# The differential layer's first values projection on the unscaled residual

## The chip, the cores and the metric

The kernel runs on one core of one Trainium2 chip. A time is the device time of one launch in microseconds (us). Profiled times come from one execution that the hardware profiler recorded. The engines are PE (TensorE: matmuls, and PEld for the loads of their stationary operand), DVE (VectorE), ACT (ScalarE), POOL (GpSimd) and SP (SyncE, whose queue issues the loads).

## What is computed

The reference is a chain of two models on 256 tokens of width 1024: a first block (two mixers and a mixture of experts), then two adaLN layers. Layer 0 has a sparse attention, layer 1 a differential attention, and each ends in a feed-forward block. Each half of a layer starts with a norm whose scale and shift come from the condition vector `c`:

```python
mod = cond @ w_ada[i] + b_ada[i]                  # six vectors of 1024 for each layer
sh1, sc1, g1, sh2, sc2, g2 = split(mod, 6)
h = rms_norm(x, ln_mix_g[i]) * (1 + sc1) + sh1
x = x + g1 * mixer(h)
h = rms_norm(x, ln_mlp_g[i]) * (1 + sc2) + sh2
x = x + g2 * (square(relu(h @ w_mlp_in[i])) @ w_mlp_out[i])
```

The differential mixer projects `h` to queries, keys and values (1024 columns each, 8 heads of 128), norms and rotates queries and keys per head of 64, takes two softmaxes per head and multiplies their weighted difference with the values. All data are fp32.

The change rests on an identity. With r the reciprocal root of one token's mean square, `h = r * (x * gain) + bias`, where `gain` and `bias` do not depend on the token. So `h @ W = r * ((x * gain) @ W) + bias @ W`: a projection can run on `x * gain` before r is known, and `bias @ W` comes out of it if `bias` is one more token.

## The kernel before

**Layout.** The residual `res` lies transposed in SBUF, 8 chunks (`KD`) of 128 features by 256 tokens. Each fp32 operand of a large product is split in a high and a low fp32r half (`hi`, `lo`), and a product is three passes: hi with hi, hi with lo, lo with hi. The activations' halves are `hT_hi` and `hT_lo`. The same memory, seen as `hX`, has 258 columns to a chunk: 256 tokens, the bias column, and a zero.

**Weights.** `load` (L131) puts 1 MB tiles into a ring of 8 slots, in program order on SP's queue. ScalarE casts the high half (`whi`, L151) and VectorE subtracts for the low half (`wlo`, L152), each 128x1024 at a time, with three buffers.

**Two forms of projection.** `proj_steps` (L461) has activations as the stationary operand and weights as the moving one: 8 chunks x 2 halves of tokens x 3 passes, 512 columns each; the result has tokens on the partitions. `proj_X_steps` (L440) has weights stationary and `hX` moving: 8 chunks x 4 blocks of 128 outputs x 3 passes, 258 columns each; the result is transposed, and its column 256 is `bias @ W`.

**Norms.** `closing` (L526) is the end of a block: for each of four pairs of chunks it adds the product to `res` times the gate, squares the result for the sums, and lets PE sum the squares over the partitions (`ssps`, `Stats.count`). There are two ways on from there.
- `Stats.rstd` and `normed`: VectorE prepares the mean, GpSimd takes the power -1/2, PE spreads the factor over the partitions (`rbps`, L358), and then each chunk is scaled (`nf`, L366), rounded to `hT_hi` (ACT, L372) and subtracted to `hT_lo` (L373). Only then can a projection start. `Stats.fill` puts adaLN products (`adaps`, L187) into PE's queue at that place.
- `Stats(plain=True)` with `feeding` (L394): each pair is written to `hX` as `res * gain` during the closing, the following product runs on it by `proj_X_steps`, `Stats.scale` makes the factor beside it as an SBUF tile `rb` and the results are scaled afterwards. Both feed-forward blocks (`mlp`, L1718) start in this way; the counts of the last two pairs and `scale` stand behind the fourth of the eight steps of their first product.

**adaLN vectors.** There are twelve, each 4 loads of 1 MB. They are made in halves on PE (`ada_half`, `fill`), or on VectorE (`ada_vector`, one load of 1 MB to a call, two operations of 128x1024, L256 and L258; after the fourth call PE sums over the partitions, 8 records). A feed-forward block calls `ada_vector` beside its products as long as fewer than `vectors` are done: 11 in the first, 12 in the second.

**The differential layer.** After the first feed-forward block, `modulated` (L2189) does the first of the two ways. `dproj(0)` (L2205) projects keys, queries and values of heads 0 to 3, in this order, each into two PSUM banks (`dps`). Norm, rope and transposes of keys and queries (`dheads`) are chains: generators that go on by one stage when a given number of projection steps has been issued. `dv` is copied from PSUM. Then `attention` runs over 8 units (heads): scores, exponentials and their difference for one unit, transposes of the weights (`ptps`, L1711) and the product with the values (`dob`) of the unit before. Into the first four units `work` puts the steps of `dproj(1)` (heads 4 to 7), and from the seventh on the first half of the output product (`oearly`); `olate` is its second half.

**Order.** Program order is priority. A planner with a simulated time line fixes the order on each engine ahead of the run; an engine then works through its queue in that order. PSUM has 8 banks, 4 of the pool `acc` and 4 of the pool `mm`.

Of the kernel before, what the change touches and what calls it, by code (L numbers as in the profile page):

```python
# [25 lines left out]
P = 128  # L26
T = 256
# [17 lines left out]
def block_kernel(ctx: ExitStack, tc: tile.TileContext, A: dict, out: bass.AP):  # L45
# [10 lines left out]
    def mm(shape=(P, 512), name="mm"):  # L56
        return mm_pool.tile(list(shape), F32, tag="mm", name=name)

    def acc(shape=(P, 512), name="acc"):
        return acc_pool.tile(list(shape), F32, tag="acc", name=name)  # L60

    def sc(shape=(P, 512), name="sc"):
        return scratch.tile(list(shape), F32, tag="sc", name=name)
# [49 lines left out]
    def col(name, i=0, n=None):  # L113
        g, r, k = where[name]
        return vcols[g][:, r + i : r + i + (k - i if n is None else n)]
# [278 lines left out]
    def feeding(gain, bias):  # L394

        hi, lo = hX
        for t in hX:
            nc.vector.memset(t.bitcast(F32)[:, :, T + 1 : TX], 0.0)
        b = bias[:, :, None]
        nc.vector.tensor_copy(hi[:, :, T : T + 1], b)  # L400
        nc.vector.tensor_tensor(lo[:, :, T : T + 1], b, hi[:, :, T : T + 1].bitcast(F32), op=ALU.subtract)

        def feed(pr):
            for k in (2 * pr, 2 * pr + 1):
                g = gain[:, k : k + 1]
                nc.scalar.activation(hi[:, k, 0:T], res[:, k, :], AF.Copy, scale=g)
                nc.vector.scalar_tensor_tensor(
                    lo[:, k, 0:T], res[:, k, :], g, hi[:, k, 0:T].bitcast(F32), op0=ALU.mult, op1=ALU.subtract
                )

        return feed
# [28 lines left out]
    def proj_X_steps(w, c0, outs):  # L440

        for k0, t in colblock(w, c0, 512):
            for k1, hi, lo in halves(t):
                for kk in range(hi.shape[1]):
                    k = k0 + k1 + kk
                    for h in range(4):
                        for i, (a, b) in enumerate(passes((hi, lo), hX)):
                            nc.tensor.matmul(  # L448
                                outs[h],
                                a[:, kk, h * P : (h + 1) * P],  # L450
                                b[:, k, :],
                                start=(k == 0 and i == 0),
                                stop=(k == KD - 1 and i == 2),
                            )
                    yield
# [70 lines left out]
    def closing(banks, gate=None, st=None, each=None, feed=None):  # L526

        def after(pr):  # L530
            v = add_pair(pr, banks[pr], gate)
            last = pr == KD // 2 - 1
            if feed is not None:
                feed(pr)
                st.square(pr, v)
                if pr >= 2:
                    st.count(pr - 2)
                return
            if st is not None:
                if last and st.w is not None:  # L540
                    held["first"]["dve"] = added[0]
                st.square(pr, v)
            if st is not None:
                for p in range(pr - 2, pr + 1 if last else pr - 1):
                    if last and p == pr and st.w is None:
                        st.fill()
                    if p >= 0:
                        st.count(p)
            if each is not None:
                for p in range(pr - 1, pr + 1 if last else pr):  # L550
                    if p >= 0:
                        each(p)

        return after
# [1084 lines left out]
    def modulation(lay, part, ln):  # L1639

        v = 6 * lay + part
        ada_until(v + 2)
        a = small.tile([P, KD], F32, tag="moda", name="moda")
        nc.vector.tensor_scalar(a, mods[v + 1], 1.0, None, op0=ALU.add)
        nc.vector.tensor_tensor(a, a, ln, op=ALU.mult)
        return a, mods[v]

    def modulated(st, lay, part, ln):
        normed(st.rstd(), *modulation(lay, part, ln))
# [68 lines left out]
    def mlp(lay, close, st, vectors):  # L1718

        ada_sum = ct("adasum", (P, D), tag="klo")  # L1720
        if ada_at[1]:
            ada_half()
        w_i, w_o = A["w_mlp_in_2"][lay], A["w_mlp_out_2"][lay]
        pend = None
        for j in range(9):
            rate[0] = 0.0
            if j < 8:
                hp = [(mm if j else acc)((P, TX), name="hp") for _ in range(4)]
                for n, _ in enumerate(proj_X_steps(w_i, j * 512, hp)):
                    if j == 0 and n == 3:  # L1730
                        st.count(2)
                        st.count(3)
                        rb = st.scale()
                both = n8("hid", F32R).rearrange("p (a k t) -> p a k t", a=2, k=4)
                for i in range(2):
                    r = sc((P, 2, T), name="relu")
                    b = pw.tile([P, 4], F32, tag="nm", name="hb")
                    for c in range(2):
                        nc.vector.tensor_copy(b[:, c : c + 1], hp[2 * i + c][:, T : T + 1])
                        nc.vector.tensor_tensor(r[:, c, :], hp[2 * i + c][:, 0:T], rb, op=ALU.mult)  # L1740
                        nc.scalar.activation(r[:, c, :], r[:, c, :], AF.Relu, bias=b[:, c : c + 1])
                    hi = both[:, 0, 2 * i : 2 * i + 2, :]
                    nc.scalar.activation(hi, r, AF.Square)
                    nc.scalar.activation(r, r, AF.Square)
                    nc.vector.tensor_tensor(both[:, 1, 2 * i : 2 * i + 2, :], r, hi.bitcast(F32), op=ALU.subtract)
                for _ in range(2):
                    if j and ada_at[0] < vectors:
                        ada_vector(ada_sum)
            if j == 0:
                banks = [acc((P, 2, T), name="mlp") for _ in range(4)]  # L1750
            if pend is not None:
                jj, bb = pend
                if jj == 7:
                    ada_close()
                    ada_until(6 * lay + 6)
                for c in (0, 2):
                    if c == 2 and ada_at[0] < vectors:
                        ada_vector(ada_sum)
                    after = close(banks) if jj == 7 and c == 2 else None
                    rows(w_o, jj * 4 + c, banks, (bb[:, 0], bb[:, 1]), c, jj == 0 and c == 0, after)  # L1760
            pend = (j, both)
# [420 lines left out]
    nlam = const.tile([P, 1], F32, name="nlam")  # L2182
    nc.vector.tensor_tensor(nlam, ls[:, 1:2], ls[:, 0:1], op=ALU.subtract)
    nc.vector.tensor_scalar(nlam, nlam, -lam_init, None, op0=ALU.add)
    st = Stats()
    mlp(0, lambda banks: closing(banks, mods[5], st), st_x, 11)


    modulated(st, 1, 0, col("lnx", 8, 8))  # L2189
    w_d = A["diff_w_in_2"][0]  # L2190
    dqT = ct("dqT", (P, KD, T), tag="t16")
    dv = ct("dv", (P, 2, D), tag="kv8")
# [3 lines left out]
    def dheads(ps, i, tabs, gain, dst, name):  # L2196
        n = ct("qn", (P, 2, 8, 64), tag=f"on{i}")
        for m in range(2):
            head_norm(ps[m], 8, n[:, m])
        rope(n, tabs, 8)  # L2200
        yield 8
        heads_T(n.rearrange("p m h d -> p m (h d)"), dst[i], gain)
        ready.add((name, i))

    def dproj(i):  # L2205

        for c0, tabs, gain, dst, name in ((1024, rt_dk, g_dk, dkT, "dk"), (0, rt_dq, g_dq, dqTs, "dq")):
            ps = [acc(name="dps") for _ in range(2)]
            yield from proj_steps(w_d, c0 + i * 512, ps)
            chains.add(dheads(ps, i, tabs, gain, dst, name))  # L2210
        ps = [acc(name="dps") for _ in range(2)]
        yield from proj_steps(w_d, 2048 + i * 512, ps)
        for m in range(2):
            nc.scalar.copy(dv[:, m, i * 512 : (i + 1) * 512], ps[m])
        ready.add(("dv", i))
# [25 lines left out]
    deps = {}  # L2241

    def diff_out(h, p):
        assert ("dv", h // 4) in ready
        pt = weights_T(p)
        yield
        j = h % 2
        if j == 0:
            dob[h // 2] = acc((P, 2, 2, P), name="dob")
        o = dob[h // 2]  # L2250
        vc = slice(h * P, (h + 1) * P)
        nc.tensor.matmul(o[:, j, 0, :], pt[:, 0:P], dv[:, 0, vc], start=(j == 0), stop=False)
        nc.tensor.matmul(o[:, j, 1, :], pt[:, P:T], dv[:, 0, vc], start=False, stop=False)
        nc.tensor.matmul(o[:, j, 1, :], pt[:, T : 3 * P], dv[:, 1, vc], start=False, stop=(j == 1))
# [91 lines left out]
```

## Time and profile before

| | us |
|---|---|
| runs: median of 3 (lowest, highest) | 1309.24 (1307.48, 1309.24) |
| the profiled execution | 1306.74 |
| its span | 1305.0 |
| PE busy | 1263.6 (97%) |
| DVE busy | 652.6 (50%) |
| ACT busy | 512.6 (39%) |
| first feed-forward block ends, first `dps` projection starts | 979.29, 988.21 |

The span is the time from the first to the last instruction in the profile. A busy share is an average over stages with different limits; what an edit is worth is read in its own stage. Matmuls are pipelined: the records of two that follow each other overlap, and the distance of their starts is what one costs PE. An fp32 matmul has two records, an fp32r matmul one. The granted clock is given as a part of the full 2.4 GHz.

### The profile page before, as it was taken

How to read it: one execution, taken by the hardware profiler on the slowest of the kernel's cores; microseconds unless marked ns; L12 is line 12 of the kernel's file. 1: busy time of each engine (PE TensorE's matmuls, PEld its weight loads, DVE VectorE, ACT ScalarE, POOL GpSimd, SP SyncE). 2: the span in 40 equal slices, each digit the busy share in tenths (PEclk: the TensorE clock that was granted, in tenths of full speed). 3: DMA queues.
4: the chain of work that ended last, by engine and by line, in shares of the span. 5: the costliest groups of instructions: out<-in, count | busy, mean ns of one | idle time of the engine just before them, and what ended most of it. 6: DMA issues, size and time to landing. Idle time of an engine off the chain costs nothing.

```text
span 1305.0 us, 22821 instructions
## 1 busy us (share of the span) xinstructions
PE 1263.6 (97%) x9471; PEld 1001.2 (77%) x9471; DVE 652.6 (50%) x1268; ACT 512.6 (39%) x918; POOL 68.4 (5%) x92
## 2 busy tenths in 40 slices
PE   8999899999999999999999999999999999999998
PEld 7779565665555555556886679999997779999998
DVE  6765310220101111105786777688766777655554
ACT  7743210111101111104555646545444565654644
POOL 1010000000000000000410000000001221000000
PEclk9999999999999999998999999999999999999999
DMA  7997799999999999998545846699677432555510
GB/s 252 369 411 302 305 421 420 420 421 421 422 420 420 421 421 421 420 413 296 186 156 193 323 140 212 206 353 338 244 256 259 161 130 76 180 173 187 194 66 33
DMA packets 99157, 373.98 MB, mean 287 GB/s; under 512 B 10649, under 2 KB 14442, under 8 KB 74730
## 3 DMA queue, kind: packets, MB, share of 16 engines
q1 hardware_dynamic: 99050, 372.49, 74.8%
q8 instruction: 76, 1.25, 0.4%
q14 instruction: 31, 0.25, 0.1%
HBM read 371.41 MB, written 1.05 MB: 285 GB/s over the span
## 4 chain that ended last, share of the span: by engine, by line
PE 74%; issue 11%; DVE 2%; ACT 1%; POOL 0%; DVEq 0%; ACTq 0%; POOLq 0%
PE hp L448 14%; PE mlp L491 14%; PE gups L1413 12%; PE dps L1443 6%; PE dps L469 5%; PE sums L1461 3%; PE gps L1367 2%; PE oearly L584 2%; PE qp L469 2%; PE olate L491 2%; PE adaps L187 1%; PE kv L469 1%; PE opair L2098 1%; PE kcv L469 1%; PE ptps L2089 1%
## 5 line engine op out<-in xcount | busy, mean ns | idle before, releaser
L152 DVE TENSOR_TENSOR wlo<-w,whi 128x1024 fp32r<-128x1024 f32 (+1 forms) x222 | 269.7, 1217 | 158.0 <-ACT whi L151 155.9
L151 ACT CAST whi<-w 128x1024 fp32r<-128x1024 f32 (+1 forms) x222 | 230.4, 1042 | 249.3 <-PE hp L448 105.6
L1413 PE MATMUL gups<-w,xg 128*64 128x256 f32 x2048 | 233.7, 381 | 3.8 <-PEq L1271 2.8
L1413 PEld LDWEIGHTS gups<-w,xg 128*64 128x64 f32 x2048 | 145.1, 137 | 90.0 <-issue 19.4
L491 PE MATMUL mlp<-hid,whi 128*128 128x256 f32 x1024 | 184.0, 282 | 0.0
L491 PEld LDWEIGHTS mlp<-hid,whi 128*128 128x128 f32 x1024 | 157.2, 188 | 0.4 <-issue 0.4
L491 PE MATMUL mlp<-hid,wlo 128*128 128x256 f32 x512 | 144.8, 283 | 0.0
L448 PE MATMUL hp<-hT_lo,whi 128*128 128x258 f32 x512 | 144.0, 282 | 0.0
L448 PE MATMUL hp<-hT_hi,whi 128*128 128x258 f32 x512 | 143.7, 283 | 0.0
L448 PE MATMUL hp<-hT_hi,wlo 128*128 128x258 f32 x512 | 142.5, 282 | 0.0
L1425 DVE TENSOR_TENSOR h<-h,gups 128x256 f32<-128x256 f32 x32 | 13.5, 421 | 235.7 <-ACT h L1424 235.7
L1443 PE MATMUL dps<-w,hT 128*64 128x512 f32 x496 | 112.7, 596 | 5.0 <-ACT hT L1433 5.0
L491 PEld LDWEIGHTS mlp<-hid,wlo 128*128 128x128 f32 x512 | 96.4, 188 | 1.6 <-issue 1.6
L448 PEld LDWEIGHTS hp<-hT_lo,whi 128*128 128x128 f32 x512 | 96.7, 189 | 0.0
L448 PEld LDWEIGHTS hp<-hT_hi,whi 128*128 128x128 f32 x512 | 96.1, 188 | 0.0
L448 PEld LDWEIGHTS hp<-hT_hi,wlo 128*128 128x128 f32 x512 | 95.9, 189 | 0.0
L1424 ACT ACTIVATE h<-gups 128x256 f32<-128x256 f32 x32 | 12.3, 383 | 181.4 <-PE gups L1413 181.4
L1443 PEld LDWEIGHTS dps<-w,hT 128*64 128x64 f32 x496 | 34.1, 137 | 64.3 <-issue 53.0
L1454 DVE COPY ysb<-dps 64x512 f32<-64x512 f32 x31 | 21.2, 683 | 107.1 <-PE dps L1443 107.0
L1455 ACT COPY ysb<-dps 64x512 f32<-64x512 f32 x31 | 18.0, 581 | 139.1 <-DVE ysb L1454 139.1
L1461 PE MATMUL sums<-sw,ysb 128*128 128x256 f32 x256 | 61.3, 385 | 6.3 <-DVE ysb L1454 6.3
L286 POOL TENSOR_TENSOR rs_r<-rs_t,mhalf 128x8 f32<-128x8 f32 (+2 forms) x24 | 36.5, 1521 | 486.4 <-DVE rs_t L280 481.3
(537 smaller groups left out, 2038.4 us busy)
## 6 DMA issues: line engine op xcount, KB each, us to landing
w<-in_w_gate_dram SPq DMA_DIRECT2D x64, 1024.0 KB
w<-in_w_up_dram SPq DMA_DIRECT2D x64, 1024.0 KB
w<-in_w_down_dram SPq DMA_DIRECT2D x62, 1024.0 KB
w<-in_w_ada_dram SPq DMA_DIRECT2D x48, 1024.0 KB
w<-in_w_mlp_in_dram SPq DMA_DIRECT2D x32, 1024.0 KB
w<-in_w_mlp_out_dram SPq DMA_DIRECT2D x32, 1024.0 KB
w<-in_diff_w_in_dram SPq DMA_DIRECT2D x12, 1024.0 KB
w<-in_w_in_dram SPq DMA_DIRECT2D x10, 1024.0 KB
```

The lines of the kernel that those rows point to most:

```text
L151: nc.scalar.copy(hi, v)
L152: nc.vector.tensor_tensor(lo, v, hi.bitcast(F32), op=ALU.subtract)
L286: nc.gpsimd.tensor_tensor(r, t, m, op=ALU.pow)
L448: nc.tensor.matmul(outs[h], a[:, kk, h * P : (h + 1) * P], b[:, k, :], start=(k == 0 and i == 0), stop=(k == KD - 1 and i == 2),)
L469: nc.tensor.matmul(outs[m], b[:, k, m * P : (m + 1) * P], a[:, kk, :], start=(k == 0 and i == 0), stop=(k == KD - 1 and i == 2),)
L491: nc.tensor.matmul(outs[dc // 2][:, dc % 2, :], a[:, 0, dc * P : (dc + 1) * P], b[:, a0 + kk, :], start=(first and kk == 0 and i == 0 and ...
L584: nc.tensor.matmul(banks[h // 2][:, h % 2, :], a[:, kk, h * P : (h + 1) * P], b[:, k, :], start=(k == 0 and i == 0 and h % 2 == 0), stop=( ...
L1367: nc.tensor.matmul(ps[:, j, :], part[:, m, k * P : (k + 1) * P], hot[:, m].rearrange("p e s -> p (e s)"), start=(n == 0), stop=(n == 3),)
L1413: nc.tensor.matmul(ps[j * 64 : (j + 1) * 64, s * 256 : (s + 1) * 256], xg[:, k, s0 : s0 + SLOTS], w[k // 4][:, k % 4, j * 256 : (j + 1) * ...
L1443: nc.tensor.matmul(dps[half * 64 : (half + 1) * 64, :], hT[:, c, j * 64 : (j + 1) * 64], dt[f // 2][:, f % 2, half * 512 : (half + 1) * 51 ...
L1454: nc.vector.tensor_copy(t[e2 * 64 : e2 * 64 + 64, 0:512], dps[0:64, :])
L1461: nc.tensor.matmul(sums[k // 2][:, k % 2, :], t[:, k * P : (k + 1) * P], sw, start=(pr == 0 and k % 2 == 0), stop=(after is not None and k ...
```

## The change

The first feed-forward block now ends as the sparse attention does: its closing feeds `res * gain` into `hX`, with the gain and bias of the differential layer's first norm. `dproj(0)` starts with the values of heads 0 to 3, by `proj_X_steps`, into two `acc` and two `mm` banks (`dvT`); behind its fourth step stand the last two counts and `scale`. Then `normed` writes `hT_hi` and `hT_lo` from `res` for the other projections. `dvalues` scales each bank by `rb` (DVE) and adds the bias column (ACT), transposes the result back in eight PE transposes, and copies it to `dv`. Keys and queries follow as before, and there is no values projection at the end of `dproj(0)`. The `fill` calls of this norm are gone with `rstd`. In `diff_out` the assertion that the values are there has become a wait of the program's order (`need`).

```diff
-    st = Stats()
-    mlp(0, lambda banks: closing(banks, mods[5], st), st_x, 11)
-    modulated(st, 1, 0, col("lnx", 8, 8))
+    st = Stats(plain=True)
+    norm_d = []
+    def close_0(banks):
+        norm_d.extend(modulation(1, 0, col("lnx", 8, 8)))
+        return closing(banks, mods[5], st, feed=feeding(*norm_d))
+    mlp(0, close_0, st_x, 11)
...
+    def dvalues(ps, rb):
+        vT = []
+        for i in range(2):
+            v = sc((P, 2, T), name="vT")
+            b = pw.tile([P, 4], F32, tag="nm", name="vb")
+            for c in range(2):
+                p = ps[2 * i + c]
+                nc.vector.tensor_copy(b[:, c : c + 1], p[:, T : T + 1])
+                nc.vector.tensor_tensor(v[:, c, :], p[:, 0:T], rb, op=ALU.mult)
+                nc.scalar.activation(v[:, c, :], v[:, c, :], AF.Identity, bias=b[:, c : c + 1])
+            vT.append(v)
+        yield 2
+        for i in range(2):
+            t = mm((P, 2, 2, P), name="tps")
+            for m in range(2):
+                for c in range(2):
+                    nc.tensor.transpose(t[:, m, c, :], vT[i][:, c, m * P : (m + 1) * P], ident)
+            nc.scalar.copy(dv[:, :, 2 * i * P : (2 * i + 2) * P].rearrange("p m (c d) -> p m c d", c=2), t)
+        ready.add(("dv", 0))
+
     def dproj(i):
+        if i == 0:
+            ps = [f((P, TX), name="dvT") for f in (acc, acc, mm, mm)]
+            for n, _ in enumerate(proj_X_steps(w_d, 2048, ps)):
+                if n == 3:
+                    st.count(2)
+                    st.count(3)
+                    norm_d.append(st.scale())
+                yield
+            rb = norm_d[2]
+            normed(rb, *norm_d[:2])
+            chains.add(dvalues(ps, rb))
         for c0, tabs, gain, dst, name in (...):
...
+        if i == 0:
+            return
         ps = [acc(name="dps") for _ in range(2)]
         yield from proj_steps(w_d, 2048 + i * 512, ps)
...
-        assert ("dv", h // 4) in ready
+        need(("dv", h // 4))
```

## Rows read from the trace of the kernel before

**Rows 1.** The page: busy us, share of the span, instructions of each engine.
```profile
PE 1263.6 (97%) x9471; PEld 1001.2 (77%) x9471; DVE 652.6 (50%) x1268; ACT 512.6 (39%) x918; POOL 68.4 (5%) x92
```

**Rows 2.** Stretches: bounds, length, busy us by engine, granted clock, DMA share, GB/s.
```profile
802.00:979.00 177.00, 176.99 (x1495) 174.07 (x1495) 133.38 (x183) 93.17 (x131) 0.00 (x0) 1.00 0.77 274
979.00:988.20 9.20, 8.25 (x88) 4.84 (x86) 5.57 (x13) 4.50 (x8) 1.62 (x1) 0.81 0.67 224
...
1034.20:1070.70 36.50, 36.50 (x183) 28.63 (x182) 29.12 (x73) 21.16 (x52) 10.28 (x5) 1.00 0.36 116
1070.70:1112.40 41.70, 39.85 (x307) 37.10 (x307) 31.77 (x77) 25.04 (x62) 3.87 (x3) 1.00 0.30 102
```

**Rows 3.** Chain of waits, 970 to 1110 us: start, us, what.
```profile
979.29 0.79 PE ssps L328 x8
...
984.01 0.90 PE rbps L358 x4
984.91 3.31 PE adaps L187 x32
988.21 29.92 PE dps L469 x128
1018.13 0.87 PE tps L391 x8
```

**Rows 4.** Groups of 979 to 988.2 us: busy us, mean ns, idle before.
```profile
L187 PE MATMUL adaps<-w,cond 128*32 128x256 f32 x64 | 5.5, 490 | 0.0
```

**Rows 5.** Time line, `olate` to first feed-forward block: start, us, what, idle before.
```profile
786.37 0.28 PE L491 MATMUL olate<-oT,wlo 128*128 128x256 f32 x1
...
796.70 1.67 POOL L286 TENSOR_TENSOR rs_r<-rs_t,mhalf 128x2 f32<-128x2 f32 x1 [109.29 <-DVE rs_t L280]
...
800.82 0.37 ACT L352 COPY rb<-rbps 128x256 f32<-128x256 f32 x1 [2.08 <-PE rbps L358]
...
801.06 0.16 DVE L1739 COPY hb<-hp 128x1 f32<-128x1 f32 x1 [0.64 <-PE hp L448]
801.22 1.42 DVE L1740 TENSOR_TENSOR relu<-hp,rb 128x256 f32<-128x256 f32 x4
```

**Rows 6.** The same before the second feed-forward block: the power.
```profile
1121.94 0.69 POOL L286 TENSOR_TENSOR rs_r<-rs_t,mhalf 128x2 f32<-128x2 f32 x1 [21.27 <-DVE rs_t L280]
```

**Rows 7.** Time line of the normed chunks before and during `dk`.
```profile
984.94 1.26 DVE L366 SCALAR_TENSOR_TENSOR nf<-res,moda,rbps 128x256 f32<-128x256 f32 x3 [1.21 <-PE rbps L358]
985.46 1.31 ACT L372 ACTIVATE hT_hi<-nf,mod 128x256 fp32r<-128x256 f32 x3 [2.92 <-DVE nf L366]
...
996.05 0.48 DVE L373 SCALAR_TENSOR_TENSOR hT_lo<-nf,mod,hT_hi 128x256 fp32r<-128x256 f32 x1
```

**Rows 8.** One `ada_vector` sum on PE; its DVE operation, min/median/max ns.
```profile
L258 DVE SCALAR_TENSOR_TENSOR adasum<-w,cond,adasum x35: 1276/1280/1289, 764.0 to 951.0; 128x1024 f32<-128x1024 f32 x35
...
837.70 0.64 PE L187 MATMUL adaps<-adasum,ones 128*32 128x256 f32 x8
```

**Rows 9.** SP's queue, 940 to 1100 us: issue, us to landing, loads.
```profile
942.71 9.99 SPq L131 DMA_DIRECT2D w<-in_w_ada_dram  x4
954.00 51.66 SPq L131 DMA_DIRECT2D w<-in_diff_w_in_dram  x12
```

**Rows 10.** Time line of `dq`'s last rope step, its transposes, scores, `ptps`.
```profile
1023.02 0.42 DVE L1671 TENSOR_TENSOR qn<-qn,rtmp 128x256 f32<-128x256 f32 x1
...
1028.11 1.03 PE L391 MATMUL tps<-ident,qn 128*128 128x128 f32 x8
...
1034.18 0.70 PE L1690 MATMUL scores<-dkT,dqT 64*128 64x256 f32 x2
...
1077.23 0.30 PE L1711 MATMUL ptps<-ident,p 128*128 128x128 f32 x1 [1.25 <-DVE deps L2231]
```

**Rows 11.** Stretches of PE alone: length, busy us, granted clock, DMA.
```profile
985.00:986.00 1.00, 1.00 (x12) 0.50 1.08 393
...
1077.00:1078.00 1.00, 0.77 (x4) 1.00 0.00 0
```

## Prediction

> **What bounds the kernel now.** I read the page's busy times first: TensorE (PE) is busy for 97% of the span [rows 1], so an edit pays only if it takes work from PE's queue or removes time in which PE waits. The table of stretches comes next [rows 2]. Inside the first feed-forward block (802 to 979 us) PE is busy for 176.99 of 177 us. Between 979.0 and 988.2 it is busy for 8.25 of 9.20 us at a mean granted clock of 0.81, and this is the stretch that the change attacks. From 1034.2 to 1070.7 PE has no idle time, and from 1070.7 to 1112.4, the later half of the attention, it has 1.85 us. The chain of waits shows what stands between the feed-forward block and the first projection [rows 3]: sums of squares, the adaLN tiles that `Stats.fill` puts there as filling, GpSimd's power, a spread of the factor, more adaLN tiles, and at 988.21 us the first `dps` matmul. By the table of groups the filling is 64 `adaps` records, 5.5 us of PE [rows 4]. So the stretch is no bare wait: 5.5 us of its 8.9 are work that has to be done somewhere.
>
> **The handover, before.** The last matmul of the block ends at 979.29 and the first projection starts at 988.21: 8.92 us. The values projection of the first heads then costs, later on, 8 x 2 x 3 = 48 matmuls; 128 of that kind took 29.92 us [rows 3], 0.234 each, so 11.2 us. Together 20.1 us.
>
> **The handover, after.** The new order is the one in which `out_late` and the first feed-forward block already meet: feeding, 96 matmuls of 258 columns, the counts inside them, the spread near their end. That place is in the trace [rows 5]. Its last `olate` matmul starts at 786.37 and by its own duration ends at 786.65; the first reader of the last bank starts at 801.06 after waiting for PE. That is 14.4 us for the 96 matmuls, 24 records of the sums and the spread, with PE in work throughout. I take 14.4 for the values projection in its new place. To it come:
> - 4 more records of the sums before the block's end (8 against 4, as `plain` counts both halves); 8 cost 0.79 us [rows 3]: +0.4.
> - The first `dk` matmul now needs a normed chunk, and that needs the factor `rb`. The copy of `rb` starts at 800.82, while the projection ends at about 801.0 [rows 5]. Copy 0.37, one `nf` (1.26/3 = 0.42) and its rounding on ScalarE (1.31/3 = 0.44 [rows 7]) make 1.2 us from the copy's start, to 802.0: PE waits 1.0 us. GpSimd's power ahead of the copy took 1.67 us there and 0.69 before the second block [rows 5, 6]; with the short one all could come 1.0 sooner, and PE would wait for nothing. I take 0.7, near the upper end, for the close of this block is the one in which the power was long.
> - Eight transposes of `vT`, 16 records: the same kind took 0.87 us for 8 [rows 3], so +1.7.
> - VectorE's pace during `dk`: before, it began the chunks 3.2 us ahead of PE (984.94 against 988.21) and wrote the last `hT_lo` by 996.5 [rows 7], about 1.5 us before PE came to that chunk. Now it starts some 2 us closer to PE and also scales four banks, 1.42 us for four in the same form [rows 5]; against that, its share of the split weights for `dk`'s first half is done during the values projection, where it is free. Between 0 and 2 us of waiting; I take 0.4.
> - The bias columns, `vb` copies and the four bias additions are on VectorE and ScalarE beside PE's 11 us of `dk`, and the two copies into `dv` replace the two of before: nothing on the path. Without that cover they would cost the four scalings' 1.4 us again.
>
> The sum: 14.4 + 0.4 + 0.7 + 1.7 + 0.4 - 20.1 = -2.5 us.
>
> **What is moved.** Without `fill`, the last of the twelve adaLN vectors is open when the diff layer ends, so the second feed-forward block makes it with `ada_vector`, as the first block did for five. Four 1 MB loads leave SP's queue between 942.71 and 952.7, ahead of the twelve loads of `diff_w_in` that begin at 954.00 [rows 9], and go in among the second block's weights. `diff_w_in` so starts four ring slots earlier, and those slots are no longer held until PE has read the adaLN tiles at 988. No row shows PE waiting for `diff_w_in`, so I count nothing. In the second block VectorE gets 8 operations, seven of 1.28 us [rows 8]; the first block carries five times that and keeps PE full [rows 2], which hides them. PE gets 8 records of 0.64 us together [rows 8]: +0.6. Were ScalarE's or VectorE's order disturbed there, it would cost up to one such operation. The total is now -1.9.
>
> **The attention.** The values projection used to be PE's work while the queries `dq` went through norm, rope and transposes: `dq`'s last rope step ends at 1023.4, its transposes run at 1028.11, the first scores at 1034.18 [rows 10]. After, the second half's projections fill that time, so 11.2 us of filling are missing further on. The 36.5 us from 1034.2 to 1070.7 have no PE idle, and VectorE is busy for 29.12 of them [rows 2]. PE's work there shrinks to 36.5 - 11.2 = 25.3 us; VectorE's must shrink by 4 as well, or it becomes the bound. It does where the splits and head norms of the second half move ahead of the first scores with their matmuls, so it fits, tightly. Bounds: a gain of the 1.85 us of idle behind it, if the second heads are ready earlier; a loss of all 11.2 if this part is paced by its latency and not by PE. I take +0.4, near the first, since PE was full there. In all **-1.5 us**.
>
> **Profile against the runs.** The profiled execution took 1306.74 us, its span 1305.0 and 1.7 around it; the median of the runs is 1309.24, 2.5 higher. The sum is a difference made in the profiled execution: 1305.2 for that one, and 1307.7 against the median.
>
> **The skill against the trace.** In 985 to 986 us the granted clock is 0.50 [rows 11], which is 1.2 GHz; PE had just run the narrow sums and waited for GpSimd's power. Around 1077, after full matmuls, a wait of 1.25 us left it at 1.00, 2.4 GHz [rows 10, 11]. The Trainium skill ("TensorE: Matmul & The Clock Gate", Part 1) says that the throttled state is the default and that activity releases it. By that rule a wait before `dk` could bring the low level back, which is the third rival below; by the row of 1077 it does not.
>
> Of the two powers (1.67 us at 796.70, 0.69 at 1121.94), the first ran beside an operation of VectorE of 1.28 us, a kind with two inputs from SBUF [rows 8]. The Trainium skill ("GPSIMD Engine Reference", Specifications) says that GpSimd shares its SBUF interfaces with VectorE and that instructions with two SBUF inputs contend; the rows agree. By the long power the wait before `dk` is 1.0 us, by the short one zero.
>
> **Rivals.**
> - *The attention gets shorter too.* The second heads' keys and queries are projected where the values were, so their norms are ready before units 4 to 7 ask. For it: 1.85 us of idle there; the transposes run 4.7 us after their data is written, so the planner's order has slack. Against: those units also wait on VectorE. Price: handover with no wait (-0.7) and no slow chunk (-0.4), and half of the idle gone with nothing lost (-1.3): -3.9 us, 1305.3.
> - *The attention runs out of filling* (slower). Eleven us of matmuls that could run at any time are gone from in front of it; when `dproj(1)` ends early, PE stands in front of `ptps` as at 1077, where it waited 1.25 us for VectorE [rows 10], but at each of six units. It decides once the added idle passes 4.5 us; six waits of 1.25 are 7.5: -1.9 + 7.5 = +5.6, 1314.8. Against: PE's idle there was zero until 1070.
> - *The clock falls at the handover.* the 3.3 us of adaLN tiles from 984.91 to 988.21 [rows 3] lie in that level; as long a stretch of `dk` at half the speed would do 1.65 us less: -1.5 + 1.65 = +0.2, 1309.4. Against: the row of 1077.
> - *It does not do what it says*: `dk` waits for all eight chunks, some 7 us at 0.9 us of VectorE each. Before, `dk` started at 988.21, 7.8 us ahead of the last chunk's write [rows 3, 7], so I give it little; it would end at 1315.
>
> **How the numbers follow.** A change under 0.2%, 2.6 us, cannot be told from none: faster is below 1306.6, slower above 1311.9. Forecast 0.42, the low clock 0.05 (both within 0.2%); the shorter attention 0.35 (faster); the lack of filling 0.14 and the waiting `dk` 0.04 (slower). That is 0.35, 0.47 and 0.18. The range, 1303.0 to 1312.5, leaves out the far half of each outer case; the forecast's own range is 1306.6 to 1310.
>
> **What would show it.** In the changed trace: no `adaps<-w,cond` and no PE idle between the block's last matmul and 96 `dvT` matmuls; `rb` copied about as these end and the first `dps` matmul within 1.2 us; granted clock 1.00 throughout; ten-odd us less between `dq`'s end and the last `dps`; eight `adaps<-adasum` records in the second block. It is wrong if PE's idle between the first scores and `olate` grows by more than 2 us, or if the first `dk` matmul waits for more than two chunks.

## The result, and the profile after

The changed kernel took 1315.82 us (median of 4 runs, 1315.23 to 1316.85) beside 1308.36 us of the kernel before on the same chip (4 runs, 1307.45 to 1309.24): ratio 1.0061, 95% interval 1.0047 to 1.0075, so 7.5 us slower by the medians and 8.0 by the ratio. I had forecast 1307.7, 1.5 less than the median that I then had (1309.24), and 1312.5 as the upper end.

The page of the changed kernel: busy us, share of the span, instructions of each engine. It answers to [rows 1].

```profile
PE 1272.2 (97%) x9483; PEld 1011.7 (77%) x9483; DVE 664.4 (51%) x1291; ACT 517.4 (39%) x931; POOL 68.7 (5%) x92
```

TensorE (PE) is as full as it was, 97%. That share doesn't show what went wrong, because a matmul at half the clock counts as busy too. The table of stretches does. First the kernel before, cut at its own milestones: the end of the first feed-forward block, the first `dps`, the first scores, the first `olate` in the chain, the end. Columns as in [rows 2].

```profile
979.30:988.20 8.90, 7.95 (x84) 4.54 (x84) 5.36 (x12) 4.50 (x8) 1.62 (x1) 0.81 0.69 232
988.20:1034.20 46.00, 46.00 (x211) 37.19 (x207) 32.31 (x48) 21.71 (x28) 7.20 (x4) 1.00 0.65 230
1034.20:1098.40 64.20, 62.95 (x377) 52.54 (x377) 49.27 (x128) 38.26 (x100) 12.29 (x7) 1.00 0.30 99
1098.40:1112.40 14.00, 13.40 (x114) 13.19 (x113) 11.62 (x23) 7.94 (x14) 1.85 (x1) 1.00 0.46 151
1112.40:1305.00 192.60, 188.32 (x1581) 187.65 (x1579) 105.02 (x158) 98.74 (x135) 0.69 (x1) 1.00 0.41 137
sum 325.70, PE 318.62 PEld 295.12 DVE 203.58 ACT 171.15 POOL 23.66; mean PE 63.72 PEld 59.02 DVE 40.72 ACT 34.23 POOL 4.73
```

The same stretches of the changed kernel:

```profile
981.90:996.40 14.50, 14.40 (x124) 14.20 (x122) 8.96 (x15) 7.23 (x11) 0.70 (x1) 1.00 0.45 147
996.40:1044.60 48.20, 47.16 (x215) 37.85 (x215) 38.58 (x69) 26.59 (x38) 13.33 (x6) 1.00 0.52 174
1044.60:1108.10 63.50, 58.55 (x335) 49.09 (x334) 48.45 (x122) 33.91 (x94) 7.46 (x6) 0.89 0.30 100
1108.10:1122.10 14.00, 13.60 (x108) 12.99 (x109) 11.61 (x23) 7.71 (x14) 0.81 (x1) 1.00 0.63 225
1122.10:1315.20 193.10, 188.73 (x1586) 187.51 (x1584) 106.82 (x158) 98.12 (x136) 1.67 (x1) 1.00 0.41 142
sum 333.30, PE 322.44 PEld 301.64 DVE 214.42 ACT 173.56 POOL 23.96; mean PE 64.49 PEld 60.33 DVE 42.88 ACT 34.71 POOL 4.79
```

Read the third row of each. PE has 48 matmuls, 11.2 us, less to do between the first scores and `olate`, and the stretch is 63.5 us long and not 64.2. Its idle time went from 1.25 to 4.95 us (length less busy; 0.47 of the 4.95 is a wait of `olate` at the end of the stretch), and its mean granted clock from 1.00 to 0.89. From the end of the block to the end of the span the changed kernel needs 333.3 us (1315.2 - 981.9), the one before 325.7: 7.6 us. The block's end itself lies 2.6 us later in this trace. 2.2 of these are there already at the last `olate` ahead of the first feed-forward block (it ends at 788.83 and at 786.65), where nothing is changed: the profiled execution of after was 1.0 above its median, that of before 1.6 below. The other 0.4 are the block, 193.1 us long and not 192.6, with its four more records of the sums. So the change costs 7.6 + 0.4 = 8.0 us by the traces.

The changed kernel's `dps` matmuls alone, ahead of the first scores and behind them:

```profile
996.37:1044.59 48.22, 45.31 (x190) 1.00 0.52 174
1044.59:1108.10 63.51, 13.85 (x51) 0.89 0.30 100
```

Before, the same count gave 190 and 99. So the planner put as many projection matmuls ahead of the first scores as it did before, and all 48 missing ones are missing behind.

What PE waited for, from the block's end into the second block: total us, times, longest.

```profile
PE ptps L1711 <- DVE dss L2308: 3.0, 1, 3.0
PE ptps L1711 <- DVE deps L2271: 1.5, 1, 1.5
PE tps L2227 <- ACT vT L2220: 1.0, 1, 1.0
PE olate L491 <- DVE wlo L152: 0.8, 2, 0.5
```

The two stops ahead of `ptps` answer to the one of 1.25 in [rows 10]. What follows them is in the stretches of PE alone (length, PE busy, granted clock, DMA):

```profile
1050.00:1051.00 1.00, 0.17 (x2) 1.00 0.05 16
1051.00:1052.00 1.00, 1.00 (x6) 0.81 0.00 0
1052.00:1053.00 1.00, 1.00 (x5) 0.50 0.08 16
...
1051.00:1059.00 8.00, 8.00 (x28) 0.57 0.01 2
1082.50:1090.00 7.50, 7.49 (x31) 0.56 0.35 128
```

Behind each stop PE is busy without a break, but for some 6.8 us at 0.50, 1.2 GHz. In the two long rows that is 8.0 x 0.43 = 3.4 and 7.5 x 0.44 = 3.3 us of work not done: more than the stops themselves. In [rows 11], after the stop of 1077, the clock had stayed at 1.00.

Why the second stop is 3.0 us long is in the chain of waits (start, us, what):

```profile
1077.79 0.62 DVE dnm L1703 x2
1078.41 0.66 DVE adasum L256
1079.07 0.53 DVE dnm L1703 x2
1079.67 1.18 DVE adasum L258
1081.05 0.60 DVE dss L2307
1081.72 0.64 DVE p L2275 x2
1082.51 0.45 PE ptps L1711
```

Two of the eight sums of the moved adaLN vector, `adasum`, stand between the maxima `dnm` and the weights `p` that `ptps` transposes. They belong to the second feed-forward block, but the planner put them into VectorE's queue here, 0.66 + 1.18 = 1.84 us on the path. Six of the eight lie in the attention, the last of them starting at 1105.57.

### The profile page after: what moved, and what is told of

The parts are those of the page before. It is cut to its first block, busy times and chain, and to the rows that moved or that the text cites. A ratio compares the mean times of both kernels' runs of the same rounds, so it can differ in the third digit from the quotient of the medians.

```text
span 1315.2 us, 22881 instructions
## 1 busy us (share of the span) xinstructions
PE 1272.2 (97%) x9483; PEld 1011.7 (77%) x9483; DVE 664.4 (51%) x1291; ACT 517.4 (39%) x931; POOL 68.7 (5%) x92
## 3 DMA queue, kind: packets, MB, share of 16 engines
q8 instruction: 76, 1.25, 0.4%
## 4 chain that ended last, share of the span: by engine, by line
PE 74%; issue 11%; DVE 2%; ACT 1%; POOL 0%; DVEq 0%; ACTq 0%; POOLq 0%
PE hp L448 14%; PE mlp L491 14%; PE gups L1413 12%; PE dps L1443 6%; PE dps L469 4%; PE sums L1461 3%; PE gps L1367 2%; PE oearly L584 2%; PE qp L469 2%; PE olate L491 2%; PE kv L469 1%; PE adaps L187 1%; PE opair L2098 1%; PE kcv L469 1%; PE ptps L2089 1%
```

## Experiments

The theory after this first reading had two parts. The attention is paced by its chain over VectorE and ScalarE, so that taking filling out of it gains nothing; and the moved sums sit in that chain. Rivals: only one of the two is true, or PE is still the bound.

**The vector late.**

```diff
-                    if j and ada_at[0] < vectors:
+                    if (j >= 5 if lay else j) and ada_at[0] < vectors:
```

The same condition went to the sum at `c == 2`.

> The changed kernel, but the second feed-forward block makes the twelfth adaLN vector from its sixth column block on, not from its second, so that no step of it can be planned into the attention. Theory (the attention is paced by its chain over VectorE and ScalarE; the moved adaLN sums sit in that chain): the 3.0 us wait ahead of ptps and the low clock behind it go, 3 to 6 us less: 1310 to 1313 us. Rival (only the filling is missing, VectorE's eight sums are harmless): 1315 to 1316 us.

1313.31 us (5 runs), beside 1307.6 of the kernel before: 1.0043 (1.0030 to 1.0056). Against the changed kernel's 1315.82 the sums in the attention cost 2.5 us (2.7 in the traces, 333.3 and 330.6 from the block's end on), and 5.7 remain without them. That is less than the 3 to 6 us of the theory, which had the low clock behind the second stop going with the sums. Its waits, its attention (first scores to first `olate`, which starts at 1106.53 in the changed kernel, after 61.9 us) and PE's stretches around the stops:

```profile
PE ptps L1711 <- DVE deps L2271: 2.7, 2, 1.5
PE tps L2227 <- ACT vT L2220: 1.0, 1, 1.0
...
```

```profile
1045.10:1105.50 60.40, 57.70 (x328) 48.80 (x328) 41.01 (x115) 32.81 (x93) 6.41 (x5) 0.89 0.21 71
...
1051.40:1059.00 7.60, 7.60 (x25) 0.55 0.01 2
1081.30:1090.00 8.70, 8.70 (x38) 0.61 0.00 0
```

The stops are 1.46 and 1.25 us now, and the low clock still follows each: 7.6 x 0.45 + 8.7 x 0.39 = 6.8 us.

**The filling put back**, with the sums where the change had them:

```diff
-        if i == 0:
-            return
         ps = [acc(name="dps") for _ in range(2)]
         yield from proj_steps(w_d, 2048 + i * 512, ps)
+        if i == 0:
+            for m in range(2):
+                nc.scalar.copy(sc(name="again"), ps[m])
+            return
```

> The changed kernel with the old projection of the first heads' values put back behind the queries, its result unused: 48 matmuls and two copies, 11.2 us of PE, nothing else. Theory (the attention is paced by latency, PE has room there): the time moves by less than 3 us, 1314 to 1318 us. Rival (the attention is bound by PE, and what was lost came from elsewhere): 1327 us.

**Both.**

> Both edits of the other two runs: the adaLN vector late, and the old projection put back as filling. Theory: the two add up, 1309 to 1313 us, and within 2 us of the run with the late vector alone though PE has 11.2 us more to do. Rival (PE bound): 1321 to 1327 us.

1324.95 us (1.0129, 1.0114 to 1.0144) and 1319.21 us (1.0088, 1.0075 to 1.0101). Both are outside what the theory allowed, and not as slow as the rival said. The 11.2 us of useless matmuls cost 9.1 and 5.9. So the attention is not simply paced by latency: PE is the bound for most of it, and filling costs its own time less what it saves. In the second run it saved the stop at unit 0 and both low clocks, 1.5 + 6.8 of the 11.2 us. That leaves 2.9; the traces differ by 4.0 from the block's end on (334.6 and 330.6), the medians by 5.9, and these runs don't say what the rest is. Its attention, first scores to `olate`:

```profile
1043.80:1109.00 65.20, 63.95 (x379) 52.90 (x379) 49.98 (x129) 37.99 (x99) 10.56 (x7) 1.00 0.30 98
```

That is the attention of the kernel before within 1 us: one stop of 1.2 us, clock 1.00. In the first run the stop of 3.0 us stayed and some 10 us at 0.50 came with it; so between these two the sums make 5.7 us, more than the 2.5 without filling, where the low clock followed the stop at unit 4 with the sums and without.

The theory was therefore changed: what the missing filling costs is the stops, and more than these the low clock behind them. If so, a little filling at the right place must pay for itself.

**Useless work in the two stops.** On top of the late vector:

```diff
+        with tc.issue_after(latest[0].ins):
+            for _ in range(14):
+                nc.tensor.transpose(ps[:, 384:512], ident, ident)
```

It stands ahead of the `ptps` transposes of units 0 and 4; `latest` is PE's last matmul of the attention.

> The run with the late adaLN vector, plus 14 transposes of the identity whose result is unread ahead of the weights' transposes of units 0 and 4, where PE stood idle for 1.46 and 1.25 us and the granted clock then fell to 0.50 for 6.5 us each; 3.1 us of useless PE work in all. Theory (each stop of PE there costs mostly by the low clock behind it, some 3.3 us): clock near 1.00 in the attention, 1306 to 1309 us. Rival (the clock falls for another reason, or only the idle time counts): 1313 us or more.

1308.35 us (12 runs; 1.0006, 0.9995 to 1.0017): 5.0 us faster than without, though PE has 3.1 us more to do.

```profile
1043.20:1098.40 55.20, 54.56 (x356) 46.70 (x356) 42.15 (x116) 32.59 (x93) 6.41 (x5) 1.00 0.23 77
```

The attention takes 55.2 us, 5.2 less than with the late vector alone (60.4), at a granted clock of 1.00. One thing is mixed in: with the dummies the planner also put the next unit's scores, some 2 us, ahead of these transposes. The next run has no such move.

**Useful work in the stops.** The changed kernel with

```diff
+    def between(ps):
+        ada_half([latest[0]])
```

at the same places, so that the vector is made on PE there.

> The changed kernel, with the twelfth adaLN vector made on PE in two halves at the same two places, as useful filling, and so no adaLN sum on VectorE after the first feed-forward block. Theory (VectorE's sums 2.5, low clock 6.5 and idle 2.7 us go, 4 us of strips come, 0.9 less in the second block): 1307 to 1309 us. Rival (the missing filling is a matter of latency that a few strips don't mend): 1312 to 1314 us.

1308.0 us (12 runs; 0.9997, 0.9987 to 1.0006): no different from the kernel before, as the theory had it. The stops are filled by strips alone, and the order of PE around them is otherwise that of the run with the late vector. PE in its attention:

```profile
1042.90:1097.90 55.00, 55.00 (x392) 45.49 (x392) 41.58 (x118) 32.76 (x93) 6.56 (x5) 1.00 0.44 154
```

The low clock is not a matter of the profiled executions alone. The granted clock averaged over the whole run, which each timed run carries, was 0.988 to 0.989 in the four runs of the changed kernel, 0.990 to 0.995 in the 75 runs of the kernel before that were taken beside the experiments, and 0.991 to 0.996 in the 24 runs of the two kernels with filled stops.

**The moved vector alone**, on the kernel before:

```diff
-            self.fill(self.last)
             rb = mm(name="rbps")
-            last = spread(r, rb[:, 0:T])
-            self.fill(last)
-            self.fill(last)
+            spread(r, rb[:, 0:T])
```

The `fill` in `closing` went too.

> The kernel before with the adaLN tiles taken out of the handover and nothing put there; the second feed-forward block makes the vector on VectorE, as in the changed kernel. It prices the moved vector alone. Theory (its sums, planned into the attention, delay the chain by 2 to 3 us, the second block takes 0.9 more, the handover gives back some 2 us): 1308 to 1311 us, with a wait of PE of more than 2 us ahead of a ptps. Rival (the sums are hidden in VectorE's idle time): 1305 to 1307 us.

1315.88 us (6 runs; 1.0057, 1.0044 to 1.0070): as slow as the whole change, and 5 us more than I had allowed. Its waits, and two of its stretches:

```profile
PE ptps L1708 <- DVE dss L2265: 3.0, 1, 3.0
PE rbps L355 <- POOL rs_r L286: 2.1, 1, 2.1
PE dps L466 <- ACT hT_hi L369: 1.1, 1, 1.1
PE tps L2274 <- DVE don L2268: 1.0, 1, 1.0
...
```

```profile
985.60:1031.00 45.40, 45.37 (x192) 36.47 (x192) 32.40 (x51) 22.00 (x29) 9.21 (x4) 0.93 0.50 162
1031.00:1103.90 72.90, 69.87 (x391) 57.44 (x391) 56.83 (x134) 39.27 (x100) 10.39 (x7) 0.95 0.39 128
```

The handover is shorter by 2.9 us, but `dk` starts in the low clock (45.4 x 0.07 = 3.2 us lost). In the attention stand the same stop of 3.0 us with sums in it and a low clock behind it (72.9 x 0.05 = 3.6 us). What I had missed is the first of these: without the adaLN tiles PE stops at the handover itself. From `olate` to the end it takes 209.6 us and not 206.6; 1.0 of that is the wait for `don`. The changed kernel doesn't pay the price at the handover, so what the moved vector costs here and what the missing filling costs there don't add.

**The vector left at the handover.** The changed kernel with

```diff
+            for _ in range(2):
+                ada_half()
             ps = [f((P, TX), name="dvT") for f in (acc, acc, mm, mm)]
```

> The changed kernel with the twelfth adaLN vector left where the kernel before had it, as 32 strips on PE at the handover (some 4 us at the full clock), ahead of the new projection; nothing else, and the order of PE in the attention stays that of the run with the late vector. Theory (the attention lacks filling whatever becomes of the vector; its two stops and their low clock cost 5 to 7 us): 1315 to 1318 us. Rival (only the vector's move cost time): 1308 to 1311 us.

1313.67 us (5 runs; 1.0041, 1.0028 to 1.0054), 1.3 below the theory's range and well above the rival's. PE's waits ahead of `ptps` are again 2.7 us in two stops. From the block's end to the first `dps`, and around the second stop, 1.25 us at unit 4:

```profile
981.50:999.80 18.30, 18.30 (x186) 16.33 (x186) 9.50 (x17) 7.14 (x10) 0.69 (x1) 1.00 0.92 328
...
1083.00:1084.00 1.00, 0.33 (x3) 1.00 0.00 0
1084.00:1085.00 1.00, 0.42 (x3) 1.00 0.00 0
1085.00:1086.00 1.00, 1.00 (x6) 1.00 0.00 0
1086.00:1087.00 1.00, 1.00 (x6) 1.00 0.00 0
```

Here no low clock followed it; the first stop, of 1.46 us, had one. One low clock less, some 3.4 us, is enough for the miss. With the vector out of the way altogether, the change still costs 6 us.

**Versions that might beat both.** First the keys, not the values, in the new form, with dv behind `dq` as filling:

```diff
-            for n, _ in enumerate(proj_X_steps(w_d, 2048, ps)):
+            for n, _ in enumerate(proj_X_steps(w_d, 1024, ps)):
...
+        yield from dheads(ts, 0, rt_dk, g_dk, dkT, "dk")
```

> The keys of the first heads, not the values, are projected on the residual without the norm's scale (scale, bias and transposes as the values had them, then head norm and rope); queries and values follow as in the kernel before, so the 11.2 us of values stay in front of the attention; the adaLN vector late. Theory: the handover's gain of about 2.5 us is kept and the queries are ready some 4 us earlier, 1304 to 1306 us. Rival (VectorE, which now has the head norm of the keys beside the eight normed chunks, paces the queries): 1308 to 1312 us.

1308.9 us (12 runs; 1.0008, 1.0000 to 1.0017), not the 1304 to 1306 of the theory. The time lies in the rival's range, but no wait of the queries for VectorE, the rival's reason, stands in its list. It waits 1.0 us for `vT`, 0.5 for ScalarE's half of a split weight, and 1.25 at unit 4, which some 3.4 us at the low clock follow:

```profile
1077.00:1078.00 1.00, 1.00 (x5) 0.76 0.00 0
1078.00:1079.00 1.00, 1.00 (x6) 0.50 0.00 0
...
1081.00:1082.00 1.00, 1.00 (x11) 1.00 0.00 0
```

The second heads' projections spread over five units, and the transposes asked for two steps later:

```diff
-        if j < 4:
-            steps(second, 7)
+        if j < 5:
+            steps(second, (7, 7, 3, 4, 6)[j])
```

> Keys first, vector late, and two changes of order: the transposes of the keys two steps later, and the second heads' projections spread over five units and not four, so that some matmuls are left where PE stood at unit 4. Theory: the 1.0 us wait and the stop with its low clock (1.3 and 2 us) go, 1304 to 1307 us. Rival (the planner puts the matmuls early all the same, another stop takes their place): 1308 to 1310 us.

1310.64 us (12 runs; 1.0021, 1.0011 to 1.0030): the rival. The planner placed the matmuls and the transposes early all the same, and the stop grew to 1.9 us, ahead of a `ptps` that waits for `p`, with 6.8 us of low clock behind it.

Then the `vT` transposes held behind a matmul, in three of the kernels:

```diff
+                    with tc.issue_after(seen[0].ins):
                         nc.tensor.transpose(t[:, m, c, :], vT[i][:, c, m * P : (m + 1) * P], ident)
```

`seen` is the last `dps` matmul issued, the twelfth here. The first two also have 4 useless transposes to a stop (the first at units 0 and 4, the second at unit 4), the third has its strips.

> The run with dummies, with 4 useless transposes in each of the two places and not 14 (2.2 us less of them), and the transposes of the values held back until 12 matmuls of the keys have been issued, so that PE no longer waits 1.0 us for ScalarE's vT. Theory: 1305 to 1307 us if PE's stops stay filled by the next unit's scores, which the planner puts there. Rival: the stops and the low clock come back, 1310 us or more.

> Keys first, vector late, the transposes held back in the same way, and 4 useless transposes at unit 4, where that kernel stopped for 1.25 us. Theory: 1.0 us of wait and some 1.8 us of low clock go, 1305 to 1307 us. Rival (another stop takes its place, as when the second heads were spread): 1308 to 1311 us.

> The run with the adaLN halves as filling in the attention, with the transposes of the values held back in the same way. Theory: the 1.0 us wait goes, 1306.5 to 1307.5 us. Rival (the values come later for unit 0, PE stops in the attention instead): 1308 to 1310 us.

1308.08 us (1.0003, 0.9994 to 1.0012), 1307.14 us (0.9993, 0.9983 to 1.0003) and 1307.09 us (0.9998, 0.9989 to 1.0008). The low clock stayed away, but the gain of 1.0 us isn't there. The third median lies in its theory's range, yet beside the kernel before it stands as it did without the edit (0.9997). The first one's waits say why:

```profile
PE dob L2305 <- ACT pt L1720: 1.7, 2, 1.0
PE dps L469 <- DVE hT_lo L373: 1.0, 1, 1.0
...
```

The wait for `vT` became a wait of the same 1.0 us for `hT_lo`, in all three kernels. VectorE writes the first `hT_lo` behind the four scalings of `vT`; in the changed kernel it is done at 998.09 us, and PE goes on at 998.15. So either product comes too late by the same time. The first kernel also waits 1.7 us for ScalarE's copy `pt`, in two stops of at most 1.0, and no low clock followed these. None of the three is faster than the kernel before by what these runs can tell.

## Why the prediction was wrong

*The handover was right.* End of block to the first `dps` was 14.5 us; I had 14.4 + 0.7 = 15.1, and 0.4 inside the block, as it came out. The projection ran without a gap, no `adaps<-w,cond` stood there, and the clock was 1.00. GpSimd's power was the short one (0.70 us), so the wait for `rb` was 0.1 and not 0.7. The pace of VectorE and ScalarE cost 1.0, as the wait for `vT`; I had 0.4 within 0 to 2. The transposes were mis-sized: [rows 3] has eight in 0.87 us, the changed kernel issues eight, and I counted 16 records, 1.7. I had taken a transpose for an fp32 matmul of two records; [rows 10] shows a `ptps` transpose with one. With 0.4 for the earlier records of the sums inside the block, that is 0.4 + 14.5 + 1.0 + 0.9 - 20.1 = -3.3 us, where I had -2.5. The stretches give much the same, 0.4 + 14.5 + 48.2 - 8.9 - 46.0 - 11.2 = -3.0.

*The step that failed is the attention*: "I take +0.4, near the first, since PE was full there." The bounds I had set, -1.85 to +11.2, held the truth near their far end. PE's work there fell by 11.2 us; 4.95 - 1.25 = 3.7 us came back as idle time and 3.4 + 3.3 = 6.7 us as low clock, 10.4 together, and the stretch became 0.7 us shorter. The sign that I had named for being wrong, over 2 us more idle between the first scores and `olate`, was there. Taken together with the handover by the stretches: -3.0 + 3.7 + 6.7 = 7.4, and 0.5 us more from `olate` to the end (207.1 against 206.6; I had 0.6 for the strips) make 7.9 of the 8.0 that the traces show.

I chose the end wrongly by arguing from PE's zero idle time from 1034 to 1070. That row says that PE was full, and 11.2 us of that fullness was what the change took out. I had read the row of VectorE beside it (29.12 us busy of 36.5) as "it fits, tightly". A sum of busy time was the wrong thing to look at: in the changed attention VectorE is busy for 48.45 of 63.5 us, and PE stops all the same, at the two places where the weights of one unit are not ready and no filling is left. And I had priced the low clock at the handover alone, in the attention at nothing.

*The second step that failed*: "In the second block VectorE gets 8 operations ... which hides them." Six of the eight ran in the attention. They cost 2.5 us by the run with the late vector. I had placed them by the line of code that issues them. In the trace they stand where their loads land: two of the six begin after VectorE has waited 0.26 and 0.99 us for a load.

*The rivals.* "The attention runs out of filling" came true, at 1314.8 against 1315.82 and with a chance of 0.14. Its price was right by luck: I had six stops of 1.25 us and no low clock; there were two stops, and low clock that cost 6.7 us. "The clock falls at the handover" had the right mechanism in the wrong place: the handover of the changed kernel has no stop, and the clock stayed at 1.00 behind the wait of 1.0 us for `vT`. I had set it aside by the row of 1077, one stop of 1.25 us at full clock. The kernels here show the same 1.25 us at unit 4 with no low clock (before, with filling and late vector, and with the vector at the handover), with some 3.4 us of it (keys first) and with 6.8 (late vector).

*What is shown and what is open.* Shown: the sums cost 2.5 us when planned into the attention of the changed kernel; the missing filling costs some 6 us without them; filling the two stops, with useless or useful work, brings the clock in the attention to 1.00 and the time back to that of the kernel before. So the change itself is worth nothing measurable: the 3.0 to 3.3 us that it saves at the handover count the adaLN strips as gone, and made on PE they take 3.8 us elsewhere (18.3 us from the block's end to the first `dps` with the vector there, 14.5 without). Open: what decides whether a stop of a given length is followed by the low clock. It never came where the stops ahead of `ptps` were filled. In the attentions of all these traces it followed each of the seven stops ahead of `ptps` that were 1.45 us or longer, and two of the five of 1.25; no run varied the length of a stop by itself.

## What to carry to other kernels

Before taking filling out of a stretch in which the bound engine also waits for a chain over other engines, list what is left to run in its stops, and price each stop with the low clock that may follow it, not with its length alone. A stop that one trace shows without that consequence doesn't rule it out. When work changes engines, look up when its inputs land: the planner may issue it far from where the code has it, into a queue that is on the path there.

## What the runs showed of the hardware

Where the low clock followed a stop of PE in the attention, the stop being 1.25 to 3.0 us long, it lasted some 3.4 us (keys first), 6.8 (most) or 10.2 (filling, with the sums), that is 1.7, 3.4 or 5.1 us of work not done. Behind the stops of 1.25 to 1.9 us the fall came only when PE was at work again: in the kernel with the late vector PE restarts at 1081.27 us, and the rows below (PE busy, granted clock) show 1.00 and 0.93 before 0.50.

```profile
1081.00:1082.00 1.00, 0.73 (x4) 1.00 0.00 0
1082.00:1083.00 1.00, 1.00 (x6) 0.93 0.00 0
1083.00:1084.00 1.00, 1.00 (x4) 0.50 0.00 0
...
1089.00:1090.00 1.00, 1.00 (x5) 0.65 0.00 0
```

PE is busy throughout those rows, so a list of waits doesn't show this loss; a table of stretches with the granted clock does. The Trainium skill ("TensorE: Matmul & The Clock Gate", Part 1) says that the throttled state is the default and that activity releases it; the fall after a stop agrees with it, and the stops without a fall are cases that the trace alone doesn't explain.
